# Sixteen of 22 gate/up pairs of a SwiGLU layer computed with Strassen's seven block products

## The chip, the cores and the metric

One NeuronCore of a Trainium2 chip. The metric is the device time of one execution in microseconds; three runs of the kernel before took 2012.99, 2013.51 and 2014.62 us, median 2013.51. All arithmetic is fp32. A product of two fp32 matrices is made on TensorE from three float32r matmuls: each operand is split into a high part and a rest, and high x high, high x rest and rest x high are summed.

## The reference, cut to what matters

Two layers of an encoder for 544 tokens (512 prompt frames and 32 sample frames) of width 1024. Each layer has a mixer (short convolution, latent attention, gated merge) and then the feed-forward part that the change touches:

```
x = x + rmsnorm(m, norm_attn_post)
gu = rmsnorm(x, norm_ffn_pre) @ w_gate_up            # (544 x 1024) @ (1024 x 5632)
f = (silu(gu[..., :2816]) * gu[..., 2816:]) @ w_down # (544 x 2816) @ (2816 x 1024)
x = x + rmsnorm(f, norm_ffn_post)
```

## The kernel before, in words

Activations lie transposed: features on the 128 partitions, tokens along the free axis, in two halves `hf` of 272 tokens (TH). 1024 features are 8 blocks of 128. A weight tile is 128 output features by 1024 inputs: 128 partitions x 1024 fp32, 512 KB. SyncE (SP) loads it into a `raw` buffer (two of them, in turn, L132), ScalarE (ACT) casts it to its high part (L129) and VectorE (DVE) subtracts to get the rest (L130); both parts are one `w` tile (L135, a ring of three, or one of the 17 big buffers of the tag "b", L78, of up to 8704 bytes per partition each).

One *unit* is one output block of 128 features for one half: `dense` (L188) issues 8 blocks x 3 matmuls = 24 matmuls of 128x128 by 128x272 (`mm3`, L183) into one PSUM bank. In this part of the kernel `psd` (L102) goes through seven banks in turn.

The order in the code: `tail(..., "mg", ...)` (L1039) makes 16 units of the merge product, eight for each half. When a half is complete, its chain `post_chain` (L317) starts: the norm over the merge product, the residual (`xb`), the unnormalised operand pair gh/gl (L341, L347), and at the end the second norm factor, which goes into `r2` (L367 to L370; then `hf` is in `ready`). The chain's steps are taken inside the following units (`step`, twice per unit of 24 matmuls), so its VectorE work stands between theirs and its few small matmuls (L237, L256) stand in TensorE's queue between units.

The gate/up part (L1066 to L1094) runs 22 pairs i, a pair being a gate tile and an up tile, each for both halves: 88 units. The first GR = 4 pairs run for half 0 and then for half 1; from there on each pair runs for both. TensorE uses the unnormalised operand; the factor r2 is multiplied in when PSUM is read: `gate` (L1046: multiply by r2, Silu), `up` (L1052: multiply by r2, multiply by the up product, cast to the high part), `low` (L1060: the rest). Units that end before their half's factor is ready are held in PSUM (`held`). `tick` (L169) after every unit splits a weight tile that has landed and has SP load the next one from the list `feed`. The results `ff` are the split operands of the down product, in groups of 8, 8 and 6 blocks.

Then `tail(..., "dn", DW, ...)` (L1102) makes 16 units of the down product, each of 22 blocks x 3 = 66 matmuls, in the order (0,0), (0,1), (1,0), ... of (m, half), reads each bank with two ScalarE instructions (square for the norm, L215, and multiply by the gain, L992), and starts the same kind of chain.

SP, GpSimd (POOL) and TensorE run in the order of the code; so do ScalarE and VectorE from L1028 on (`manual_schedule`). POOL has no work in the gate/up part beside four DMAs that store the residual (L336).

Of the kernel before, what the change touches and what calls it, by code (L numbers as in the profile page):

```python
# [33 lines left out]
def kernel(  # L34
# [67 lines left out]
    def psd(n=512):  # L102
        tag = "d"
        if wide[0]:
            tag = "dstdstd"[turn[0] % 7]
            turn[0] += 1
        return bank(tag)[:, :n]

    def f32(ap):
        return ap.bitcast(F32)  # L110
# [203 lines left out]
        stages(NW, scale, low)  # L314
        return hi, lo

    def post_chain(pre_l, pre_key, m, acc, xb, x_dst, gaps, hf, full=None, raw=None, scales=None):  # L317
        def pause(i):
            for _ in range(gaps[i]):
                yield  # L320

        yield from pause(0)
        d = rsqrt_cols([(acc, FS, EPS)])[0]
        yield from pause(1)
        r = bcast(d)
# [124 lines left out]
    for l in range(NL):  # L450
# [516 lines left out]
                dve.tensor_add(sg[hf], sg[hf], tg[hf][:, m, :])  # L967
                split(mxb[hf][0][:, m, :], mxb[hf][1][:, m, :], sg[hf])

        def tail(units, key, widths, rhs, l, post_key, pre_l, pre_key, x_src, x_dst, gaps, outs):  # L970
            mres = [blk([P, NC, TH], F32, "m") for _ in range(2)]
            accs = [Acc(), Acc()]
            ws = {}
            left = [NC, NC]
            for n, (m, hf) in enumerate(units):
                left[hf] -= 1
                ps = psd(TH)
                for pi, wdt in enumerate(widths):
# [24 lines left out]

        done = set()
        last = l == NL - 1
        GR = 4
        DW = (1024, 1024, 768)

        def after(*u):
            return lambda: u in done  # L1010

        def w_g(j, gate):
            return ("gu", j), w_gu[l, j], 1024, gate

# [5 lines left out]
        feed += [w_g(j, None) for j in range(2 * GR, 2 * FFC)]  # L1020
        for m in (0, 1, 2, 3, 4, 5, 6, 7, 5):
            feed += w_d(m, None if m != 6 else after("dn", 3, 0))
        if not last:
            feed += [(("in", l + 1, m), w_in[l + 1, m], 1024, after("dn", 7, 0) if m < 8 else None) for m in range(10)]
# [7 lines left out]
        for _ in range(3):  # L1032
# [2 lines left out]
        load_next()  # L1035
        now[0] += 1
        units = [(m, hf) for hf in range(2) for m in range(8)]
        h2, ready = {}, set()
        tail(units, "mg", (1024,), lambda hf, pi: mxb[hf], l, "attn_post", l, "ffn_pre",  # L1039
                  lambda hf: xs[hf], lambda hf: x_mid[l][hf], GM,  # L1040
                  [dict(raw=h2, scales=(r2, ready))] * 2)

        ff = [[(blk([P, n, TH], F32R, "fh"), blk([P, n, TH], F32R, "fl")) for n in (8, 8, 6)] for _ in range(2)]
        wg, held, sls, lows = {}, [], {}, []

        def gate(i, hf, ps):  # L1046
            sl = small([P, TH], s="sl")
# [4 lines left out]
        def up(i, hf, ps):  # L1052
            sl = sls[(i, hf)]
            dve.tensor_mul(sl, sl, r2[:, hf, :])
            dve.tensor_mul(sl, sl, ps)  # L1055
            fh, fl = ff[hf][i // 8]
            act.copy(fh[:, i % 8, :], sl)  # L1057
            lows.append((fl[:, i % 8, :], sl, fh[:, i % 8, :]))

        def low():  # L1060
            while lows:
                o, x, hi = lows.pop(0)
                dve.tensor_sub(o, x, f32(hi))

        runs = [(i, hf) for hf in range(2) for i in range(GR)] + [(i, hf) for i in range(GR, FFC) for hf in range(2)]
        for n, (i, hf) in enumerate(runs):  # L1066
            while hf not in h2:
                step()
            pss = []
            for u in range(2):  # L1070
                if (i, u) not in wg:
                    wg[(i, u)] = claim(("gu", 2 * i + u))
                ps = psd(TH)
                dense(ps, wg[(i, u)], h2[hf], NC)
                if hf == 1 and not 3 <= 2 * i + u < 2 * GR:
                    free[0] += 1
                low()
                pss.append(ps)
                if hf in ready:
                    while held:  # L1080
                        a = held.pop(0)
                        gate(a[0], a[1], a[2][0])
                        up(a[0], a[1], a[2][1])
                        low()
# [6 lines left out]
                tick()  # L1091
            if (i, hf) not in sls:
                held.append((i, hf, pss))
        low()  # L1094
# [7 lines left out]
        tail(units, "dn", DW, lambda hf, pi: ff[hf][pi], l, "ffn_post", l + 1, None if last else "attn_pre",  # L1102
             lambda hf: x_mid[l][hf], lambda hf: y_out[hf] if last else x_end[hf], GD, outs)
        if last:
            drain()
            vec.__exit__(None, None, None)
# [94 lines left out]
```

## Time and profile before

| | |
|---|---|
| median of the runs | 2013.51 us |
| profiled execution, its time | 2012.29 us |
| its span | 2010.4 us |
| TensorE busy | 1980.8 us, 15516 matmuls |
| VectorE, ScalarE, GpSimd busy | 1130.5, 826.1, 86.1 us |
| DMA | 190.89 MB, mean 95 GB/s |

Busy times are sums over the span; a matmul's record overlaps the next one's, so the pace of TensorE is read from the starts of matmuls and not from the durations (about 290 ns) of the records. A line number in a row can be a helper's: L129/L130 are all splits, L184 to L186 all matmul triples. A timeline row gives start, duration, engine, line and, in brackets, the idle time before it and what ended that.

### The profile page before, as it was taken

How to read it: one execution, taken by the hardware profiler on the slowest of the kernel's cores; microseconds unless marked ns; L12 is line 12 of the kernel's file. 1: busy time of each engine (PE TensorE's matmuls, PEld its weight loads, DVE VectorE, ACT ScalarE, POOL GpSimd, SP SyncE). 2: the span in 40 equal slices, each digit the busy share in tenths (PEclk: the TensorE clock that was granted, in tenths of full speed). 3: DMA queues.
4: the chain of work that ended last, by engine and by line, in shares of the span. 5: the costliest groups of instructions: out<-in, count | busy, mean ns of one | idle time of the engine just before them, and what ended most of it. 6: DMA issues, size and time to landing. Idle time of an engine off the chain costs nothing.

```text
span 2010.4 us, 37143 instructions
## 1 busy us (share of the span) xinstructions
PE 1980.8 (99%) x15516; PEld 1958.1 (97%) x15516; DVE 1130.5 (56%) x2318; ACT 826.1 (41%) x1676; POOL 86.1 (4%) x212
## 2 busy tenths in 40 slices
PE   8999999999999999999999999999999999999997
PEld 8999999999999999999999999999999999999997
DVE  7877776534457444432568777854344664444234
ACT  5455555612353222322445555555123533222231
POOL 0100000000000000000100100100000000000000
PEclk9999999999999999999999999999999999999999
DMA  5122222222342222223532222222223412222233
GB/s 194 63 77 68 69 82 69 92 98 85 112 154 87 79 91 85 85 88 88 193 106 78 75 69 72 81 91 79 85 94 119 158 55 93 87 94 83 79 107 135
DMA packets 58887, 190.89 MB, mean 95 GB/s; under 512 B 7968, under 2 KB 9664, under 8 KB 58592
## 3 DMA queue, kind: packets, MB, share of 16 engines
q1 hardware_dynamic: 49104, 163.58, 24.2%
q0 software_dynamic: 8320, 22.66, 3.5%
q8 instruction: 121, 1.98, 0.4%
q10 hardware_dynamic: 1296, 2.29, 0.3%
q14 instruction: 46, 0.38, 0.1%
HBM read 174.11 MB, written 10.20 MB: 92 GB/s over the span
## 4 chain that ended last, share of the span: by engine, by line
PE 92%; DVE 4%; DMA 1%; ACT 1%; issue 1%; DVEq 0%; SPq 0%; ACTq 0%
PE ps_d L184 16%; PE ps_d L186 16%; PE ps_d L185 16%; PE ps_s L184 7%; PE ps_s L186 7%; PE ps_s L185 7%; PE ps_t L184 6%; PE ps_t L186 6%; PE ps_t L185 6%; PE ps_t L755 2%; DMA raw<-in_w_in 1%; PE ps_v L770 1%; DVE w L130 1%; PE ps_v L771 1%; ACT w L129 1%
## 5 line engine op out<-in xcount | busy, mean ns | idle before, releaser
L130 DVE TENSOR_TENSOR w<-raw,w 128x1024 fp32r<-128x1024 f32 (+4 forms) x317 | 363.8, 1148 | 442.6 <-ACT w L129 441.2
L129 ACT CAST w<-raw 128x1024 fp32r<-128x1024 f32 (+4 forms) x317 | 312.1, 986 | 271.1 <-PE ps_d L186 98.6
L184 PE MATMUL ps_d<-hh,w 128*128 128x272 f32 x1096 | 320.0, 292 | 1.3 <-DVE v L130 1.3
L185 PE MATMUL ps_d<-hl,w 128*128 128x272 f32 x1096 | 317.0, 289 | 0.8 <-DVE hl L311 0.8
L186 PE MATMUL ps_d<-hh,w 128*128 128x272 f32 x1096 | 317.3, 290 | 0.0
L184 PE MATMUL ps_d<-gh,w 128*128 128x272 f32 x704 | 206.3, 293 | 6.1 <-DVE w L130 6.0
L184 PEld LDWEIGHTS ps_d<-hh,w 128*128 128x128 f32 x1096 | 206.9, 189 | 3.0 <-PE ps_d L186 1.7
L185 PEld LDWEIGHTS ps_d<-hl,w 128*128 128x128 f32 x1096 | 206.8, 189 | 2.0 <-DVE hl L311 1.3
L186 PEld LDWEIGHTS ps_d<-hh,w 128*128 128x128 f32 x1096 | 206.6, 189 | 0.0
L186 PE MATMUL ps_d<-gh,w 128*128 128x272 f32 x704 | 204.7, 291 | 0.0
L185 PE MATMUL ps_d<-gl,w 128*128 128x272 f32 x704 | 203.8, 289 | 0.0
L184 PEld LDWEIGHTS ps_d<-gh,w 128*128 128x128 f32 x704 | 133.5, 190 | 6.7 <-DVE w L130 6.5
L184 PE MATMUL ps_t<-gh,w 128*128 128x272 f32 x464 | 135.0, 291 | 0.0
L186 PE MATMUL ps_t<-gh,w 128*128 128x272 f32 x464 | 134.2, 289 | 0.0
L185 PEld LDWEIGHTS ps_d<-gl,w 128*128 128x128 f32 x704 | 133.8, 190 | 0.0
L185 PE MATMUL ps_t<-gl,w 128*128 128x272 f32 x464 | 133.6, 288 | 0.0
L186 PEld LDWEIGHTS ps_d<-gh,w 128*128 128x128 f32 x704 | 133.5, 190 | 0.0
L184 PE MATMUL ps_s<-gh,w 128*128 128x272 f32 x432 | 125.4, 290 | 0.1
L186 PE MATMUL ps_s<-gh,w 128*128 128x272 f32 x432 | 125.0, 289 | 0.0
L185 PE MATMUL ps_s<-gl,w 128*128 128x272 f32 x432 | 124.4, 288 | 0.0
L1049 ACT ACTIVATE sl<-sl 128x272 f32<-128x272 f32 x88 | 38.0, 432 | 182.1 <-DVE sl L1048 182.1
L1057 ACT CAST fh<-sl 128x272 fp32r<-128x272 f32 x88 | 36.9, 420 | 160.5 <-DVE sl L1055 160.5
(331 smaller groups left out, 5343.0 us busy)
## 6 DMA issues: line engine op xcount, KB each, us to landing
raw<-in_w_in SPq DMA_DIRECT2D x91, 512.0 KB, 3.3
raw<-in_w_gu SPq DMA_DIRECT2D x88, 512.0 KB, 3.2
raw<-in_w_mix SPq DMA_DIRECT2D x48, 512.0 KB, 3.2
raw<-in_w_dn SPq DMA_DIRECT2D x36, 512.0 KB, 3.6
raw<-in_w_dn SPq DMA_DIRECT2D x18, 384.0 KB, 3.0
raw<-in_w_b SPq DMA_DIRECT2D x16, 320.0 KB, 2.9
x_mid<-xb POOLq DMA_DIRECT2D x16, 272.0 KB, 2.3
xb<-x_mid POOLq DMA_DIRECT2D x16, 272.0 KB, 4.7
```

What stands on the lines that cost most here:

```text
L129: act.copy(hi, src)
L130: dve.tensor_sub(lo, src, f32(hi))
L184: pe.matmul(ps, lhsT=wlo, rhs=xhi, start=first, stop=False)
L185: pe.matmul(ps, lhsT=whi, rhs=xlo, start=False, stop=False)
L186: pe.matmul(ps, lhsT=whi, rhs=xhi, start=False, stop=last)
L755: pe.transpose(pt[:, o * P : o * P + P], probs[qt][:, kt * P : kt * P + P], ident)
L770: pe.matmul(out, lhsT=both, rhs=ptl[:, b, o : o + 256], start=kt == 0, stop=False)
L771: pe.matmul(out, lhsT=both, rhs=pth[:, b, o : o + 256], start=False, stop=kt == nkt - 1)
L1049: act.activation(sl, sl, AF.Silu)
L1057: act.copy(fh[:, i % 8, :], sl)
```

## The change

For 16 of the 22 pairs of each layer (i = 6 to 21; GN = 6), the four units of a pair (gate and up, two halves) are seen as one product of 2 x 2 blocks: outputs (gate, up) x (half 0, half 1), summed over two halves k0, k1 of the 1024 features. Eight block products of 4 blocks x 3 matmuls become seven, with sums of operand blocks made beforehand and sums of results made afterwards (the variant with shared sums).

- Operands x: `x_forms` makes the normalised operand in place in `xb` (kept by `keep`), from it four sums T1 to T4, and splits seven blocks of 128 x 4 x 272 (B11, B21, B22, T1 to T4) once per layer, in steps that are put behind the units of the first pairs from run n = 3 on, two steps per unit.
- Weights: `w_load(b)` has SP load six 256 KB blocks for a pair (four into a buffer `ra`, one into half a raw buffer, one into `u1`), and POOL add to three of them by accumulating DMAs; the third of these reads what the first has written. `produce` splits them to 3.5 `w` tiles of 1024 columns for the next pair; one more sum is made by VectorE. The load for a pair is issued two to three pairs ahead.
- Results: one copy, seven VectorE additions or subtractions of 272 columns from PSUM, one Silu and one multiplication of 544 columns per pair, in place of gate/up/low. Results are kept unsplit in `fx` and split later: four splits of 544 columns in the last pair, the other seven of half 0 ahead of the first down unit, all eleven of half 1 ahead of the second (`f_splits`, called by `tail` through `before`).
- The loads of the down weights are issued in the last two pairs; before, `tick` issued them.
- The first six pairs run as before, without `low` and with their product written to `fx`.

```diff
-        GR = 4
+        GR, GN = 4, 6
+        fx = [blk([P, 4, 2, TH], F32, "fx") for _ in range((FFC + 3) // 4)]
         def up(i, hf, ps):
             sl = sls[(i, hf)]
             dve.tensor_mul(sl, sl, r2[:, hf, :])
-            dve.tensor_mul(sl, sl, ps)
-            fh, fl = ff[hf][i // 8]
-            act.copy(fh[:, i % 8, :], sl)
-            lows.append((fl[:, i % 8, :], sl, fh[:, i % 8, :]))
+            dve.tensor_mul(fx[i // 4][:, i % 4, hf, :], sl, ps)
+        def form(name, k, src):
+            if name not in xf:
+                xf[name] = blk([P, 2, 4, TH], F32R, "xf")
+            hi, lo = xf[name][:, 0, k : k + 2, :], xf[name][:, 1, k : k + 2, :]
+            act.copy(hi, src)
+            while later:
+                later.pop(0)()
+            later.append(lambda: dve.tensor_sub(lo, src, f32(hi)))
+        def w_load(b):
+            def src(u, half):
+                return w_gu[l, 2 * (GN + b) + u, :, 512 * half : 512 * half + 512]
+            ra = blk([P, 2048], F32, "ra")
+            g0, s3, s2, s1 = [ra[:, o : o + 512] for o in range(0, 2048, 512)]
+            nc.sync.dma_start(s1, src(1, 0))
+            nc.sync.dma_start(s3, src(1, 0))
+            nc.sync.dma_start(s2, src(0, 0))
+            nc.sync.dma_start(g0, src(0, 0))
+            nc.gpsimd.dma_start(s1, src(1, 1), accum_op=ALU.add)
+            nc.gpsimd.dma_start(s3, src(0, 0), accum_op=ALU.add)
+            nc.gpsimd.dma_start(s2, s1, accum_op=ALU.add)
+            rb = rawp.tile([P, 1024], F32, tag=ring("raw", 2), name=nm("raw"))
+            nc.sync.dma_start(rb[:, 0:512], src(0, 1))
+            u1 = tmp([P, 512], s="u1")
+            nc.sync.dma_start(u1, src(1, 1))
+        def produce(n):
+            b, j = n // 4, n % 4
...
+            if j == 2:
+                dve.tensor_add(rb[:, 512:1024], ra[:, 1024:1536], rb[:, 0:512])
+            src = (ra[:, 0:1024], ra[:, 1024:2048], rb, u1)[j]
+            wd = 512 if j == 3 else 1024
+            w = wt[n] = w_tile(n % 5 < 2 or b == NB - 1)
+            act.copy(w[:, 0, :wd], src)
+            while wlater:
+                wlater.pop(0)()
+            wlater.append(lambda: dve.tensor_sub(w[:, 1, :wd], src, f32(w[:, 0, :wd])))
...
+            if j == 2 and b + 2 < NB:
+                w_load(b + 2)
+        order = ("B11", "T3", "T2", "T1", "B21", "B22", "T4")
+        for b in range(NB):
+            i = GN + b
+            sl, up2 = tmp([P, 2, TH], s="slp"), tmp([P, 2, TH], s="upp")
+            for f in range(7):
+                n = 4 * b + f // 2
+                ps = banks[f] = psd(TH)
+                w, o = wt[n], 512 * (f % 2)
+                x = xf[order[f]]
+                for k in range(4):
+                    s = slice(o + k * P, o + k * P + P)
+                    mm3(ps, w[:, 0, s], w[:, 1, s], x[:, 0, k, :], x[:, 1, k, :], k == 0, k == 3)
+                if f == 0:
+                    act.copy(sl[:, 0, :], ps)
+                elif f == 2:
+                    dve.tensor_sub(sl[:, 1, :], sl[:, 0, :], ps)
+                    dve.tensor_add(up2[:, 0, :], sl[:, 1, :], banks[1])
...
+                elif f == 5:
+                    dve.tensor_add(sl[:, 1, :], sl[:, 1, :], ps)
+                    act.activation(sl, sl, AF.Silu)
+                elif f == 6:
+                    dve.tensor_add(up2[:, 0, :], up2[:, 0, :], ps)
+                    dve.scalar_tensor_tensor(fx[i // 4][:, i % 4, :, :], up2, -1.0, sl, op0=ALU.mult, op1=ALU.mult)
+                if f in (1, 3, 5, 6):
+                    produce(n + 4)
...
+        def f_splits(m, hf):
+            while todo and todo[0][0] == hf:
+                f_split(*todo.pop(0))
```

## Rows read from the trace of the kernel before

**Rows 1.** The page: span, then busy time, share and instructions of each engine.
```profile
span 2010.4 us, 37143 instructions
PE 1980.8 (99%) x15516; PEld 1958.1 (97%) x15516; DVE 1130.5 (56%) x2318; ACT 826.1 (41%) x1676; POOL 86.1 (4%) x212
```
**Rows 2.** Waits of TensorE: who, for whom, us in total, times, longest.
```profile
PE ps_d L184 <- DVE w L130: 6.0, 1, 6.0
...
PE ps_v L256 <- DVE y L250: 2.5, 2, 1.9
```
**Rows 3.** Windows: gate/up part of layer 0 (busy us of each engine, PEclk, DMA share, GB/s).
```profile
597.00:870.00 273.00, 273.00 (x2170) 273.00 (x2169) 139.98 (x270) 87.17 (x151) 2.17 (x4) 1.00 0.25 87
```
**Rows 4.** Timeline of TensorE: two units' first matmuls, a chain's transposes, the down part's start.
```profile
601.96 0.29 PE L184 MATMUL ps_d<-gh,w 128*128 128x272 f32 x1
...
604.99 0.29 PE L184 MATMUL ps_s<-gh,w 128*128 128x272 f32 x1
...
640.26 0.49 PE L256 MATMUL ps_v<-ident,y 128*128 128x128 f32 x3
...
867.58 0.29 PE L184 MATMUL ps_s<-fh,w 128*128 128x272 f32 x1
```
**Rows 5.** Groups by line and form on VectorE: count, busy us, mean ns, idle before.
```profile
L130 DVE TENSOR_TENSOR w<-raw,w 128x1024 fp32r<-128x1024 f32 x263 | 322.0, 1225 | 418.9 <-ACT w L129 417.5
...
L347 DVE SCALAR_TENSOR_TENSOR gl<-xb,gn,gh 128x272 fp32r<-128x272 f32 x40 | 18.2, 495 | 0.0
...
L1055 DVE TENSOR_TENSOR sl<-sl,ps_d 128x272 f32<-128x272 f32 x39 | 17.1, 438 | 14.7 <-PE ps_d L186 12.4
...
L130 DVE TENSOR_TENSOR xl<-at,xh 128x544 fp32r<-128x544 f32 x16 | 10.7, 714 | 12.4 <-ACT xh L129 12.4
...
L130 DVE TENSOR_TENSOR w<-raw,w 128x512 fp32r<-128x512 f32 x8 | 5.5, 688 | 0.0
```
**Rows 6.** The same on ScalarE.
```profile
L129 ACT CAST w<-raw 128x1024 fp32r<-128x1024 f32 x263 | 274.9, 1046 | 247.4 <-PE ps_d L186 78.8 <-PE ps_t L186 45.7 <-PE ps_s L186 40.9
L1049 ACT ACTIVATE sl<-sl 128x272 f32<-128x272 f32 x88 | 38.0, 432 | 182.1 <-DVE sl L1048 182.1
...
L129 ACT CAST xh<-z 128x544 fp32r<-128x544 f32 x16 | 9.2, 642 | 0.0
...
L129 ACT CAST w<-raw 128x512 fp32r<-128x512 f32 x8 | 5.0, 621 | 3.7 <-PE ps_d L186 3.7
```
**Rows 7.** Timeline of VectorE after the second half's chain, layer 0.
```profile
626.53 0.43 DVE L1063 TENSOR_TENSOR fl<-sl,fh 128x272 fp32r<-128x272 f32 x1
...
634.20 0.15 DVE L239 TENSOR_SCALAR v<-ps_d 128x3 f32<-128x3 f32 x1
```
**Rows 8.** DMA queues in 681:850 (169 us): packets, MB, share of 16 engines.
```profile
q1 hardware_dynamic: 4011, 14.64, 25.0%
```
**Rows 9.** DMA queues in 584:609 (25 us), where POOL's DMAs run too.
```profile
q1 hardware_dynamic: 797, 2.94, 33.3%
q0 software_dynamic: 640, 2.23, 24.1%
```
**Rows 10.** DMA issues over the span: queue, count, KB each, median us to landing.
```profile
raw<-in_w_gu SPq DMA_DIRECT2D x88, 512.0 KB, 3.2
...
xb<-x_mid POOLq DMA_DIRECT2D x16, 272.0 KB, 4.7
...
xb<-in_x POOLq DMA_DIRECT2D x8, 272.0 KB, 3.8
...
raw<-in_w_a SPq DMA_DIRECT2D x8, 256.0 KB, 2.8
```
**Rows 11.** Timeline of POOL: the issue of a DMA.
```profile
619.13 0.55 POOL L336 DMA_DIRECT2D x_mid<-xb  x1 [0.72 <-DVE xb L335]
```
**Rows 12.** Timeline of ScalarE at the end of the first down unit.
```profile
876.11 0.40 ACT L215 ACTIVATE sq<-ps_s 128x272 f32<-128x272 f32 x1 [6.16 <-PE ps_s L186]
876.40 0.48 ACT L992 ACTIVATE m<-ps_s,gn 128x272 f32<-128x272 f32 x1
```
**Rows 13.** Windows: near the span's end, TensorE with a gap (columns as in rows 3).
```profile
1995.00:2000.00 5.00, 3.64 (x29) 3.34 (x27) 0.77 (x3) 0.78 (x2) 0.00 (x0) 1.00 0.00 0
```

More of the change, by code (lines that the diff above doesn't have):

```diff
@@ L315, in norm_split, with post_chain @@
         return hi, lo
-    def post_chain(pre_l, pre_key, m, acc, xb, x_dst, gaps, hf, full=None, raw=None, scales=None):
+    def post_chain(pre_l, pre_key, m, acc, xb, x_dst, gaps, hf, full=None, raw=None, scales=None, keep=None):
         def pause(i):
@@ L367, in post_chain @@
         if raw is not None:
+            if keep is not None:
+                keep[hf] = xb
             t, r = r, scales[0][:, hf, :]
@@ L968, with tail @@
                 split(mxb[hf][0][:, m, :], mxb[hf][1][:, m, :], sg[hf])
-        def tail(units, key, widths, rhs, l, post_key, pre_l, pre_key, x_src, x_dst, gaps, outs):
+        def tail(units, key, widths, rhs, l, post_key, pre_l, pre_key, x_src, x_dst, gaps, outs, before=None):
             mres = [blk([P, NC, TH], F32, "m") for _ in range(2)]
@@ L977, in tail @@
                 ps = psd(TH)
+                if before is not None:
+                    before(m, hf)
                 for pi, wdt in enumerate(widths):
@@ L1019 @@
         feed += [w_g(j, None) for j in range(3)] + [w_g(j, after("mg", j, 1)) for j in range(3, 2 * GR)]
[L1020 to L1024, printed above, removed]
+        feed += [w_g(j, None) for j in range(2 * GR, 2 * GN)]
         xs = x0 if l == 0 else x_end
@@ L1037 @@
         units = [(m, hf) for hf in range(2) for m in range(8)]
-        h2, ready = {}, set()
+        h2, ready, keep = {}, set(), {}
         tail(units, "mg", (1024,), lambda hf, pi: mxb[hf], l, "attn_post", l, "ffn_pre",
                   lambda hf: xs[hf], lambda hf: x_mid[l][hf], GM,
-                  [dict(raw=h2, scales=(r2, ready))] * 2)
-        ff = [[(blk([P, n, TH], F32R, "fh"), blk([P, n, TH], F32R, "fl")) for n in (8, 8, 6)] for _ in range(2)]
-        wg, held, sls, lows = {}, [], {}, []
+                  [dict(raw=h2, scales=(r2, ready), keep=keep)] * 2)
+        fx = [blk([P, 4, 2, TH], F32, "fx") for _ in range((FFC + 3) // 4)]
+        wg, held, sls = {}, [], {}
         def gate(i, hf, ps):
@@ L1054, in up @@
             dve.tensor_mul(sl, sl, r2[:, hf, :])
-            dve.tensor_mul(sl, sl, ps)
-            fh, fl = ff[hf][i // 8]
-            act.copy(fh[:, i % 8, :], sl)
-            lows.append((fl[:, i % 8, :], sl, fh[:, i % 8, :]))
[L1060 to L1065, printed above, removed]
+            dve.tensor_mul(fx[i // 4][:, i % 4, hf, :], sl, ps)
@@ new lines, with x_forms, quarter @@
+        xf = {}
+        later = []
+        def form(name, k, src):
[6 more added lines that the diff above has]
+            later.append(lambda: dve.tensor_sub(lo, src, f32(hi)))
+        def x_forms():
+            def quarter(hf, half, k):
+                return keep[hf][:, 4 * half + k : 4 * half + k + 2, :]
+            for hf in range(2):
+                while hf not in ready:
+                    yield False
+                for half in range(2):
+                    for k in (0, 2):
+                        q = quarter(hf, half, k)
+                        for e in range(2):
+                            c = 4 * half + k + e
+                            dve.scalar_tensor_tensor(q[:, e, :], q[:, e, :], g(l, "ffn_pre", c), r2[:, hf, :],
+                                                     op0=ALU.mult, op1=ALU.mult)
+                        if hf == 0 or half == 1:
+                            form(("B11", "B21", "", "B22")[2 * hf + half], k, q)
+                        yield True
+            b11, b21, b12, b22 = [lambda k, hf=hf, half=half: quarter(hf, half, k) for hf in range(2) for half in range(2)]
+            for name, o, x, y, op in (("T1", b11, b11, b12, ALU.subtract), ("T3", b12, b22, b12, ALU.subtract),
+                                      ("T2", b22, b22, b11, ALU.add), ("T4", b21, b22, b21, ALU.subtract)):
+                for k in (0, 2):
+                    dve.tensor_tensor(o(k), x(k), y(k), op=op)
+                    form(name, k, o(k))
+                    yield True
+            while later:
+                later.pop(0)()
@@ new lines @@
+        NB = FFC - GN
+        wt, rws = {}, {}
+        wlater = []
+        def w_load(b):
[14 more added lines that the diff above has]
+            nc.sync.dma_start(u1, src(1, 1))
+            rws[b] = ra, rb, u1
@@ new lines, in produce @@
+        def produce(n):
+            b, j = n // 4, n % 4
+            if b >= NB:
+                return
+            ra, rb, u1 = rws[b]
+            if j == 2:
[7 more added lines that the diff above has]
+            wlater.append(lambda: dve.tensor_sub(w[:, 1, :wd], src, f32(w[:, 0, :wd])))
+            if n == 4 * NB - 1:
+                wlater.pop(0)()
+            if j == 2 and b + 2 < NB:
+                w_load(b + 2)
@@ L1066 @@
+        runs = [(i, hf) for hf in range(2) for i in range(GR)] + [(i, hf) for i in range(GR, GN) for hf in range(2)]
+        xg = x_forms()
+        xdone, xq = [False], [0]
         for n, (i, hf) in enumerate(runs):
@@ L1076 @@
                     free[0] += 1
-                low()
                 pss.append(ps)
@@ L1083 @@
                         up(a[0], a[1], a[2][1])
-                        low()
                     if u == 0:
@@ L1091 @@
                 tick()
+                d = 2 * n + u - 4 * GR
+                if n >= GR - 1:
+                    for _ in range(2):
+                        if next(xg, None) is None:
+                            break
+                if d == 1:
+                    w_load(0)
+                if d == 5:
+                    w_load(1)
+                if d in (3, 5, 6, 7):
+                    produce(xq[0])
+                    xq[0] += 1
             if (i, hf) not in sls:
                 held.append((i, hf, pss))
-        low()
+        for _ in xg:
+            pass
@@ new lines, with f_split @@
+        while chains:
+            step()
+        for m in (0, 1, 2, 3, 4, 5, 6, 7, 5):
+            feed += w_d(m, None if m != 6 else after("dn", 3, 0))
+        if not last:
+            feed += [(("in", l + 1, m), w_in[l + 1, m], 1024, after("dn", 7, 0) if m < 8 else None) for m in range(10)]
+        ff = [[(blk([P, n, TH], F32R, "fh"), blk([P, n, TH], F32R, "fl")) for n in (8, 8, 6)] for _ in range(2)]
+        def f_split(hf, gi, k):
+            s = slice(k, k + 2)
+            split(ff[hf][gi][0][:, s, :], ff[hf][gi][1][:, s, :], fx[2 * gi + k // 4][:, k % 4 : k % 4 + 2, hf, :])
@@ new lines @@
+        todo = [(hf, gi, k) for hf in range(2) for gi, n in enumerate((8, 8, 6)) for k in range(0, n, 2)]
+        order = ("B11", "T3", "T2", "T1", "B21", "B22", "T4")
+        for b in range(NB):
+            i = GN + b
+            sl, up2 = tmp([P, 2, TH], s="slp"), tmp([P, 2, TH], s="upp")
+            banks = {}
+            for f in range(7):
[11 more added lines that the diff above has]
+                    dve.tensor_add(up2[:, 0, :], sl[:, 1, :], banks[1])
+                elif f == 3:
+                    dve.tensor_add(up2[:, 1, :], up2[:, 0, :], ps)
+                    dve.tensor_add(sl[:, 1, :], sl[:, 1, :], ps)
+                elif f == 4:
+                    dve.tensor_add(sl[:, 0, :], sl[:, 0, :], ps)
+                elif f == 5:
+                    dve.tensor_add(sl[:, 1, :], sl[:, 1, :], ps)
+                    act.activation(sl, sl, AF.Silu)
[4 more added lines that the diff above has]
+                    produce(n + 4)
+                e = f if b == NB - 1 else -1
+                if b == NB - 2 and f in (4, 6) or e in (1, 4, 6):
+                    load_next()
+                if e in (0, 3, 5):
+                    split_next()
+                if e in (1, 2, 4, 5):
+                    f_split(*todo.pop(0))
@@ L1096 @@
+        free[0] = 0
+        def f_splits(m, hf):
+            while todo and todo[0][0] == hf:
+                f_split(*todo.pop(0))
         units = [(m, hf) for m in range(5) for hf in range(2)] + [(5, 0), (6, 0), (7, 0), (7, 1), (6, 1), (5, 1)]
@@ L1102 @@
         tail(units, "dn", DW, lambda hf, pi: ff[hf][pi], l, "ffn_post", l + 1, None if last else "attn_pre",
-             lambda hf: x_mid[l][hf], lambda hf: y_out[hf] if last else x_end[hf], GD, outs)
+             lambda hf: x_mid[l][hf], lambda hf: y_out[hf] if last else x_end[hf], GD, outs, f_splits)
         if last:
```

## The prediction, as it was put on record before the result

> **What bounds the kernel now.** I read the page's engine shares first: TensorE is busy 1980.8 of 2010.4 us, VectorE 56%, ScalarE 41% [rows 1]. Busy time alone doesn't say that TensorE sets the time, so the second view is TensorE's waits. The longest single wait is 6.0 us, at the start; after that none is over 1.9 us [rows 2]. Third, the stage that the change touches: in the gate/up part of layer 0 TensorE never pauses in 273 us, at a granted clock of 1.00 (2.4 GHz), with VectorE at 140.0 us (51%) and the DMA engines at a share of 0.25 [rows 3]; layer 1's window is the same within 1 us. So here a matmul removed is time removed, as long as nobody else becomes late. The price of a matmul comes from starts, not from the overlapping records: two units of 24 matmuls begin at 601.96 and 604.99, 3.03 us a unit, 0.126 us a matmul [rows 4].
>
> **The change part by part.**
>
> *Matmuls.* A pair is 4 units, 4 x 3.03 = 12.12 us. Afterwards it is seven products of 12 matmuls, each half a unit: 7 x 1.515 = 10.6 us. Saved: 1.515 us x 16 pairs x 2 layers = 48.5 us. Shape, operand kinds and bank rotation stay, so I take the same price per matmul. That is all the change can give.
>
> *VectorE and ScalarE in the pair loop.* Per pair VectorE has three rests of 1024 columns (3 x 1.225), a rest and a sum of 512 (2 x 0.688), seven 272-column operations on PSUM (7 x 0.438) and one of 544 columns (0.714): 8.8 us of 10.6 [rows 5]. Before it was 2 x 1.225 + 8 x 0.438 = 6.0 of 12.1. ScalarE has 3 x 1.046 + 0.621 + a copy (0.43) + a Silu of 544 columns (0.64) = 4.8 us [rows 6]. Neither is over, so the question is order. A `w` tile's rest is issued four to five products (6.1 us or more) before TensorE wants it. Walking one pair with these durations, TensorE at 1.515 us a product: the second tile's rest stands behind the additions of product 5 and ends 11.5 us after the pair's start, wanted at 13.6; the third ends at 13.8, wanted at 16.7; the first ends at 8.4, wanted at 10.6. So about 2 us to spare, a PSUM bank is read long before its turn comes again seven products later, and the cost is 0. If that cover went, TensorE would run at VectorE's pace (rival 2).
>
> *Operand forms.* Per layer, on VectorE 16 x 0.495 + 8 x 0.714 + 14 x 0.714 = 23.6 us [rows 5], on ScalarE 14 x 0.642 = 9.0 us [rows 6], put between the evictions of units 6 to 18 of the 24 that remain ahead of the pair loop (counted from 0), where TensorE has work of its own. The tight place is half 0's four steps behind units 6 and 7 (n = 3). They stand in VectorE's queue ahead of the small chain that half 1's second norm needs, which starts at 634.20 [rows 7] and takes 1.7 us; TensorE wants its result for the transposes at 640.26 [rows 4], and these can't be passed. The steps are 8 x 0.495 + 4 x 0.714 = 6.8 us; three `low` of 0.44 (one at 626.53 [rows 7]) and the two waits of half a microsecond before them go. End of the chain: 634.2 + 1.7 + 6.8 - 2.3 = 640.4 by mean durations, some 2 us sooner if back-to-back instructions overlap. Cost 0 to 1.6 us per layer; I take 0, because instructions that stand side by side on one engine do overlap in the trace, by 0.11 us in the one pair shown [rows 12]. From unit 12 on VectorE gets 2.2 to 4.9 us per 3.03 us unit and falls behind by at most 4 us; seven banks give it 18.
>
> *Weights.* SP moves 6 x 262 KB = 1.57 MB per pair instead of 1.05. At 14.64 MB in 25.0% of 169 us = 346 GB/s [rows 8] that is 4.5 us of all 16 DMA engines. The trace has no accumulating DMA. Lower end: the price of POOL's plain DMAs, 2.23 MB in 24.1% of 25 us = 370 GB/s [rows 9]: 0.79 MB in 2.1 us, together 6.6 of 10.6 us. Upper end: each has all engines for its whole time to landing, 4.7 us in the worst plain row [rows 10]: 14.1 us, together 18.6. I take twice the plain price, 4.2 us, since such a transfer has to read two operands where a plain one reads one and the row of POOL's plain DMAs is the nearest [rows 9]: 8.7 us per pair, 82% of the DMA engines, cost 0. Latency: load, first accumulation, accumulation on that one, 2.8 + 3.8 + 3.8 = 10.4 us by [rows 10], 14 if each is slowed to 4.7. The load is issued behind product 5 of one pair and wanted behind product 1 or 3 of the pair after next, 15 to 18 us later. POOL's issue is 3 x 0.55 us per pair [rows 11] on an idle engine. The waits that POOL gets hold up only its own next accumulation.
>
> The Trainium skill (DMA: Bandwidth & Descriptors, section Rules for kernel authors) says that an accumulating DMA reads its destination and writes it later, which is what the doubled price stands for; no run here shows it yet. The same page (section Anatomy of one DMA) gives each DMA a fixed 2.0 us beside its bytes. If the fixed part occupied the engines, nine DMAs of 262 KB would be an estimated 9 x 2.6 = 23 us a pair. The trace disagrees as far as plain loads go: a 512 KB load lands in 3.2 us, yet costs the engines 1.5 us by the rate above [rows 8].
>
> *Start of the down part.* Before, its operands were split long ahead. Now half 1's eleven splits stand behind the first down unit's two reads on ScalarE. That unit ends 8.31 us after its start, at 875.89 (867.58 plus 66 x 0.126), and ScalarE's reads of it end at 876.88 [rows 4, 12], 1.0 us later; then a cast (0.64) and a rest (0.71) must end before the second matmul of unit (0,1): 2.4 us of idle TensorE. From there a split covers 6 matmuls (0.76 us) and takes 0.64 to 0.71, so it keeps ahead. The next weight tile's split stands behind all eleven: 1.0 + 11 x 0.64 + 1.05 + 1.23 = 10.3 us after unit (0,0)'s end, unit (1,0) starts 2.4 + 8.3 = 10.7 after it: just in time. Half 0's seven splits run at 0.7 us each against 0.76 and start with 3 us of lead: 0. So 2.4 us x 2 layers = 4.8 us lost; ends 0 and 4 us per layer. The clock: the row nearest to such a gap has TensorE idle for 1.4 us and still at 1.00 [rows 13].
>
> *Sum*, against the profiled execution's 2012.29 us: -48.5 + 4.8 = -43.7, 1968.6 us. The median of the runs stands 1.2 us above that execution: **1970 us**.
>
> **Rivals.**
>
> 1 (slower). *Accumulating DMAs are several times dearer than plain ones and the DMA engines become the bound.* Place: the pair loop from the third pair on, when the lead of two pairs is used up: 14 pairs x 2 layers. At four times the plain price: 4.5 + 8.5 = 13.0 us per pair, 2.4 over 10.6, 67 us in all: 2037 us. It decides from 12.2 us per pair (43.7 / 28 over 10.6), an accumulation of 2.5 us, 3.6 times plain. For it: the operation is new here, and per-pair DMA time at least rises from 3.0 to 6.6 us. Against: plain DMAs leave the engines three quarters idle [rows 3].
>
> 2. *VectorE's order, not its sum, sets the pair's pace.* A 2 us margin is small when an instruction reads PSUM right behind TensorE. If a pair takes VectorE 11.3 us (8.8 of work, and 2.5 of waits that it can't fill, for the bank, for Silu and for the cast), 0.7 x 32 = 22 us are lost: 1992 us. For it: in the gate/up part VectorE's busy groups show waits of 0.3 us and more per instruction for ScalarE and TensorE [rows 5]. Against: in my walk it idles only once per pair, about 1 us.
>
> 3. *Fixed costs per DMA occupy the engines.* Worked from rows as a mechanism here: each 262 KB load taking its 2.8 us to landing in turn [rows 10] would give 6 x 2.8 = 16.8 us a pair before any accumulation, 6.2 over, 174 us lost: 2144 us. The page's fixed 2.0 us (above) is this case. The rate of 346 GB/s speaks against it [rows 8].
>
> **How the numbers follow.** My forecast has 0.67, its own range 1963 to 1978 (nothing lost at the down part, or 4 us per layer and 1.6 per layer in the forms). Rival 2, or a milder DMA bound that leaves a gain, 0.12: 1980 to 2006. Rival 1: 0.16, rival 3: 0.02; the rest, 0.03, lies near no change. Range 1962 to 2006, which leaves out about 0.2, nearly all of it above. A measurement of this kernel tells a difference from about 0.2%, 4 us. Faster 0.79, same 0.03, slower 0.18.
>
> **What will show it.** 384 matmuls fewer in each engine row and 0.126 us still between starts; TensorE's waits by name: `w` from VectorE or a DMA on `ra` in the pair loop (rivals 1 to 3), VectorE on `fl` at the second down unit, 2 to 3 us, twice. DMA share in the pair loop near 0.8; at 0.95 or more rival 1 has come true. VectorE near 85% there; above 95% it is rival 2. The prediction is wrong if the pair takes more than 10.8 us.

## The result, and the profile after

The changed kernel takes 1985.3 us (median of 4 runs, 1983.2 to 1990.3) against 2013.3 us before on the same chip (2012.8 to 2014.6): a ratio of 0.9864, 95% interval 0.9844 to 0.9883. It is faster, by 28 us. The forecast was 1970 us with a loss of 4.8 us against a gain of 48.5: the time lies in the range of 1962 to 2006, outside of the forecast's own 1963 to 1978. So 16 us of the forecast gain are to be found, or 20.5 us of the full 48.5. The profiled execution below is the slowest of the four, 1990.3 us with a span of 1988.5, so it shows some 5 us more of loss than the median.

The page of the changed kernel, span and engines (answers to [rows 1]):

```profile
span 1988.5 us, 37200 instructions
...
PE 1944.8 (98%) x15132; PEld 1919.9 (97%) x15132; DVE 1264.9 (64%) x2510; ACT 889.3 (45%) x1724; POOL 171.1 (9%) x308
```

The 384 matmuls are gone, yet TensorE's busy time fell by only 36.0 us and the span by 21.9. Busy time that doesn't fall with the count is matmuls that became longer, so the clock is to be looked at too. The same window as in [rows 3], and within it the pair loop alone, which runs from 679.86 to 849.35 (busy us of each engine, granted clock, DMA share, GB/s):

```profile
597.00:870.00 273.00, 267.19 (x2080) 266.10 (x2079) 210.00 (x369) 121.04 (x179) 44.47 (x52) 0.98 0.67 167
680.00:849.00 169.00, 169.00 (x1343) 169.00 (x1342) 130.28 (x209) 72.55 (x96) 36.10 (x41) 1.00 0.83 200
```

In the pair loop TensorE never pauses. The losses lie in front of it and behind it. TensorE's waits inside the window 597:870 (answers to [rows 2]):

```profile
PE ps_s L184 <- DVE w L130: 2.8, 1, 2.8
PE ps_s L184 <- ACT fh L129: 1.4, 1, 1.4
PE ps_d L185 <- DVE fl L130: 1.2, 2, 0.7
PE ps_s L185 <- DVE fl L130: 0.4, 1, 0.4
```

Layer 1 has the same four groups (2.9, 1.4, 1.1 and 0.4 us). Where the span's time went is read from the first matmul on each kind of operand: `gh` opens the gate/up part, `fh` the down part. In the timeline of TensorE, before:

```profile
598.94 0.29 PE L184 MATMUL ps_t<-gh,w 128*128 128x272 f32 x1
...
1594.90 0.29 PE L184 MATMUL ps_d<-gh,w 128*128 128x272 f32 x1
...
1863.53 0.29 PE L184 MATMUL ps_d<-fh,w 128*128 128x272 f32 x1
```

and after:

```profile
599.16 0.29 PE L184 MATMUL ps_t<-gh,w 128*128 128x272 f32 x1
...
849.35 0.29 PE L184 MATMUL ps_d<-fh,w 128*128 128x272 f32 x1
...
1585.68 0.29 PE L184 MATMUL ps_d<-gh,w 128*128 128x272 f32 x1
...
1835.86 0.29 PE L184 MATMUL ps_s<-fh,w 128*128 128x272 f32 x1
```

The differences of these starts (with 867.58 of [rows 4], and those of the experiments read in the same way) split each span into five stretches:

| us | to first gh | gate/up 0 | down 0 to gate/up 1 | gate/up 1 | down 1 to the end | span |
|---|---|---|---|---|---|---|
| before | 598.9 | 268.6 | 727.3 | 268.6 | 146.9 | 2010.4 |
| after | 599.2 | 250.2 | 736.3 | 250.2 | 152.6 | 1988.5 |
| e1_pace | 599.0 | 246.1 | 731.6 | 246.2 | 152.7 | 1975.5 |
| e2_early | 598.8 | 249.0 | 729.6 | 249.2 | 148.9 | 1975.5 |
| e3_both | 599.1 | 246.1 | 728.9 | 245.9 | 148.9 | 1968.9 |
| e4_fill | 600.1 | 247.7 | 731.4 | 247.7 | 151.1 | 1978.0 |
| e5_noacc | 598.3 | 249.1 | 734.7 | 248.8 | 151.1 | 1982.0 |

Each gate/up part should have become shorter by 16 x 1.515 = 24.2 us and became 18.4 shorter: 5.8 us lost per layer. The down parts grew by 9.0 and 5.8 us where 2.4 was forecast. The row of e5_noacc, an experiment below with the same order of work, is a second look at the changed kernel: that execution took 1983.8 us, near the median, and lost 4.7 and 4.4 us in the gate/up parts and 7.4 and 4.2 behind them.

**The place in the gate/up part.** The one wait on `w` from L130 is that of unit 21, the up tile of pair 5, the last but two of the ordinary units. ScalarE, VectorE and TensorE there (timelines; the bracket is the idle time before and its releaser):

```profile
665.32 0.43 ACT L1049 ACTIVATE sl<-sl 128x272 f32<-128x272 f32 x1 [0.34 <-DVE sl L1048]
665.66 1.03 ACT L129 CAST w<-raw 128x1024 fp32r<-128x1024 f32 x1
```
```profile
664.22 0.72 DVE L1067 TENSOR_TENSOR xf<-xb,xf 128x544 fp32r<-128x544 f32 x1
664.86 0.43 DVE L1048 TENSOR_TENSOR sl<-ps_s,r 128x272 f32<-128x272 f32 x1
666.72 1.23 DVE L130 TENSOR_TENSOR w<-raw,w 128x1024 fp32r<-128x1024 f32 x1 [1.43 <-ACT w L129]
```
```profile
658.96 0.29 PE L184 MATMUL ps_t<-gh,w 128*128 128x272 f32 x1
...
668.00 0.60 PE L184 MATMUL ps_s<-gh,w 128*128 128x272 f32 x1 [2.83 <-DVE w L130]
...
673.61 0.43 PE L184 MATMUL ps_t<-gh,w 128*128 128x272 f32 x1
```

Read from the bottom: unit 18 ends where the next one starts, at 658.96, but VectorE comes to read it only at 664.86, 5.9 us later, because the steps that make the operand forms (L1067 and the lines before it) stand ahead. ScalarE's Silu (L1049) waits for that, and in ScalarE's queue the cast of unit 21's weight tile stands behind the Silu. Then VectorE's rest of the tile must follow: TensorE waits 2.83 us. With ScalarE's cast, VectorE's rest and the two gate operations (1.03 + 1.23 + 0.43 + 0.43 = 3.1 us) the tile would have been ready at 665.17, where the unit before it ended, if VectorE had been 3.1 us late and not 5.9: the difference is the wait.

The wait isn't all. The 24 matmuls behind it last from 668.00 to 673.61, 5.6 us for 3.03. The windows there:

```profile
666.00:668.00 2.00, 0.00 (x0) 0.00 (x1) 1.28 (x2) 1.63 (x2) 0.21 (x1) 0.80 0.91 288
668.00:670.00 2.00, 2.00 (x9) 2.00 (x10) 1.72 (x4) 0.14 (x1) 1.55 (x2) 0.50 0.81 230
670.00:674.00 4.00, 4.00 (x19) 4.00 (x19) 0.60 (x2) 1.23 (x2) 0.00 (x0) 0.50 0.80 162
674.00:676.00 2.00, 2.00 (x18) 2.00 (x17) 1.42 (x2) 0.00 (x0) 0.12 (x1) 0.99 0.92 215
```

The granted clock falls to 0.50, the lower of TensorE's two levels (1.2 GHz), after TensorE had stood still, and returns at 674. That is 2.6 us more; 2.8 + 2.6 = 5.4 of the 5.8 lost in this execution.

**The place at the start of the down part.** TensorE's matmuls that waited, and ScalarE's queue that answers to [rows 12]:

```profile
852.40 0.39 PE L185 MATMUL ps_d<-fl,w 128*128 128x272 f32 x1 [0.49 <-DVE fl L130]
...
854.14 0.39 PE L185 MATMUL ps_d<-fl,w 128*128 128x272 f32 x1 [0.73 <-DVE fl L130]
...
860.97 0.39 PE L184 MATMUL ps_s<-fh,w 128*128 128x272 f32 x1 [1.40 <-ACT fh L129]
861.73 0.58 PE L185 MATMUL ps_s<-fl,w 128*128 128x272 f32 x1 [0.37 <-DVE fl L130]
```
```profile
859.60 0.40 ACT L215 ACTIVATE sq<-ps_d 128x272 f32<-128x272 f32 x1 [4.51 <-PE ps_d L186]
859.90 0.48 ACT L996 ACTIVATE m<-ps_d,gn 128x272 f32<-128x272 f32 x1
860.27 6.11 ACT L129 CAST fh<-fx 128x544 fp32r<-128x544 f32 x11
```

By the starts of the matmuls around them the two `fl` waits on half 0's splits cost 1.5 us and the pair at 861 costs 2.2 us. The latter is the forecast step, mechanism and size (2.4). The former was costed at nothing. After it, too, the clock is at half for a while:

```profile
862.00:864.00 2.00, 2.00 (x10) 2.00 (x10) 2.00 (x4) 2.00 (x5) 0.00 (x0) 0.50 0.00 0
864.00:866.00 2.00, 2.00 (x14) 2.00 (x13) 2.00 (x4) 2.00 (x5) 0.00 (x0) 0.70 0.04 8
```

From 861.73 to 865.24 stand 15 intervals that would take 1.9 us and took 3.5: 1.6 us. Together 5.3 us per layer.

**A third place.** What is left of layer 0's 9.0 us lies around the start of layer 1, where nothing was changed. From the third unit of the down part to the first `gh` of layer 1 it is 710.7 us before, 714.1 after and 714.0 in e5_noacc: 3.3 to 3.5 us lost in both. TensorE waits there once for 3.7 us on `y` (L256), where it waited 0.6 before, and the clock is at half twice (0.57 on average over 981:985 and over 1008:1012) where it was once before. In e1_pace to e4_fill the same stretch takes 710.6 to 711.2 us, although none of them edits it, in e6_moreacc and e7_more 712.1 and 712.5. Why it depends on the order of work ahead of it was not followed.

**DMA.** The queues in 700:820, where every pair loads for a later one (packets, MB, share of 16 engines; answers to [rows 8, 9]):

```profile
q1 hardware_dynamic: 9910, 18.04, 47.4%
q0 software_dynamic: 4803, 8.73, 44.6%
```

The accumulating queue moved 8.73 MB in 44.6% of 120 us, 163 GB/s, 2.27 times as dear as the plain 370 of [rows 9]; SP's loads ran at 317 GB/s for 346. The share is 0.92 in this stretch, and still TensorE has no wait in the pair loop, on a transfer or on a weight tile.

### The profile page after: what moved, and what is told of

Read it like the earlier page. It is cut to its first block, busy times and chain, and to the rows that moved or that the text cites. A ratio compares the mean times of both kernels' runs of the same rounds, so it can differ in the third digit from the quotient of the medians.

```text
span 1988.5 us, 37200 instructions
## 1 busy us (share of the span) xinstructions
PE 1944.8 (98%) x15132; PEld 1919.9 (97%) x15132; DVE 1264.9 (64%) x2510; ACT 889.3 (45%) x1724; POOL 171.1 (9%) x308
## 4 chain that ended last, share of the span: by engine, by line
PE 84%; DVE 10%; DMA 2%; ACT 2%; issue 2%; SPq 0%; DVEq 0%; ACTq 0%
PE ps_d L184 15%; PE ps_d L185 15%; PE ps_d L186 15%; PE ps_s L184 6%; PE ps_s L185 6%; PE ps_s L186 6%; PE ps_t L184 5%; PE ps_t L186 5%; PE ps_t L185 5%; PE ps_t L757 2%; DVE w L130 2%; DMA raw<-in_w_in 2%; ACT w L129 1%; PE ps_v L772 1%; PE ps_v L773 1%
## 5 line engine op out<-in xcount | busy, mean ns | idle before, releaser
L130 DVE TENSOR_TENSOR w<-raw,w 128x1024 fp32r<-128x1024 f32 (+5 forms) x253 | 285.4, 1129 | 328.1 <-ACT w L129 326.8
L129 ACT CAST w<-raw 128x1024 fp32r<-128x1024 f32 (+5 forms) x253 | 245.4, 971 | 269.8 <-PE ps_d L186 103.1
L184 PE MATMUL ps_d<-xf,w 128*128 128x272 f32 x384 | 111.3, 290 | 0.0
L186 PE MATMUL ps_d<-xf,w 128*128 128x272 f32 x384 | 111.1, 289 | 0.0
L185 PE MATMUL ps_d<-xf,w 128*128 128x272 f32 x384 | 110.6, 288 | 0.0
L744 ACT ACTIVATE pr<-ps_s,y 128x128 f32<-128x128 f32 (+3 forms) x128 | 67.6, 528 | 69.3 <-DVE y L741 67.4
L185 PE MATMUL ps_d<-fl,w 128*128 128x272 f32 x308 | 88.9, 289 | 1.2 <-DVE fl L130 1.2
L184 PE MATMUL ps_d<-fh,w 128*128 128x272 f32 x308 | 89.6, 291 | 0.0
L186 PE MATMUL ps_d<-fh,w 128*128 128x272 f32 x308 | 89.1, 289 | 0.0
L184 PE MATMUL ps_d<-gh,w 128*128 128x272 f32 x248 | 73.8, 298 | 6.2 <-DVE w L130 6.2
L1132 DVE TENSOR_TENSOR w<-ra,w 128x1024 fp32r<-128x1024 f32 x64 | 78.0, 1219 | 0.0
L184 PE MATMUL ps_s<-xf,w 128*128 128x272 f32 x256 | 74.2, 290 | 0.0
L184 PE MATMUL ps_t<-xf,w 128*128 128x272 f32 x256 | 74.2, 290 | 0.0
L186 PE MATMUL ps_s<-xf,w 128*128 128x272 f32 x256 | 74.1, 289 | 0.0
L186 PE MATMUL ps_t<-xf,w 128*128 128x272 f32 x256 | 74.1, 289 | 0.0
```

The costliest lines, as they stand in the source:

```text
L129: act.copy(hi, src)
L130: dve.tensor_sub(lo, src, f32(hi))
L184: pe.matmul(ps, lhsT=wlo, rhs=xhi, start=first, stop=False)
L185: pe.matmul(ps, lhsT=whi, rhs=xlo, start=False, stop=False)
L186: pe.matmul(ps, lhsT=whi, rhs=xhi, start=False, stop=last)
L744: act.activation(pr[:, :nk], ps[:, :nk], AF.Exp, bias=mx, accum_out=sm)
```

## The experiments

My theory after this reading: two queue positions cost two waits per layer, each followed by half clock, and the DMAs cost nothing. The main rival: the accumulating DMAs, with which the engines are at 0.92, delay something that the waits don't show. The experiments ran on two chips on which the kernel before took 2014.2 to 2014.4 us, 1 us more than above, and four runs of one kernel spread over 2 to 7 us, so the differences of medians below are good to some 3 us.

**e1_pace: the forms later.** Two form steps per unit from the time on that their inputs are there become a written-out map by unit.

```
+PACE = {6: 2, 7: 2, 12: 2, 13: 2, 14: 2, 15: 2, 16: 1, 18: 2, 19: 1, 20: 1}
-if n >= GR - 1:
-    for _ in range(2):
-        if next(xg, None) is None:
-            break
+for _ in range(PACE.get(2 * n + u, 0)):
+    next(xg, None)
```

> Theory A: the gain is lost at two places per layer, each a wait of TensorE and then a stretch at half clock. Place 1 is the up tile of pair 5, whose split stands behind operand forms in VectorE's queue: 2.8 us of wait and 24 matmuls at 0.227 us for 0.126, 2.4 us more. Here the forms leave room (one step behind unit 16, none behind 17, the rest behind 18 to 20), so the wait goes: about 2 x 5.2 = 10 us less than the changed kernel, 1975 us, with place 2 unchanged. Rival B: TensorE only meets here what the pair loop's DMAs and VectorE would make it wait for anyway; the first pairs' weights then come late, since xb's buffer comes free some 5 us later, and the time stays within 3 us of the changed kernel.

1977.4 us (1976.1 to 1980.4), ratio to before 0.9819 [0.9804, 0.9833]: 7.8 us off the changed kernel's median, nearer to theory A than to B. TensorE's waits in 597:870, the window at unit 21, and ScalarE ahead of the new wait:

```profile
PE ps_t L184 <- DVE w L1132: 1.4, 1, 1.4
PE ps_s L184 <- ACT fh L129: 1.4, 1, 1.4
```
```profile
668.00:672.00 4.00, 4.00 (x34) 4.00 (x33) 3.52 (x7) 2.87 (x4) 0.55 (x1) 1.00 0.61 176
```
```profile
686.79 1.05 ACT L1129 CAST w<-ra 128x1024 fp32r<-128x1024 f32 x1 [3.82 <-DMA ra<-ra]
```

The wait of unit 21 and its half clock are gone; each gate/up part is 4.0 us shorter than in the changed kernel's profile, and 2.6 to 3.0 shorter than in e5_noacc's. The other part of the 7.8 us lies at the third place, which this edit doesn't touch. A smaller wait takes the old one's place: L1132 is the rest of a pair's weight tile, here of pair 1. Its loads are issued at 667.94, 6.0 us ahead of the pair loop, where the changed kernel issues them 15.5 us ahead (664.38), and by the trace's releaser its cast waits for the landing of the third accumulating DMA (`ra<-ra`). So with the forms later, TensorE does wait behind a pair's DMAs, 1.4 us a layer.

**e2_early: half 1's splits ahead of the first down unit.**

```
-if e in (1, 2, 4, 5):
+if e in (1, 2, 3, 4):
     f_split(*todo.pop(0))
 ...
-while todo and todo[0][0] == hf:
+while todo:
     f_split(*todo.pop(0))
```

> Theory A: place 2 is the start of the down part: 3.0 us of waits for fl and fh and a stretch at half clock after them, about 2 us. Here all splits stand ahead of the first down unit's eviction on ScalarE, and the four of the last pair one product earlier: 2 x 4 to 5 us less, 1975 to 1977 us, with place 1 unchanged. Rival B: the splits are bound by VectorE's total work there, so the wait moves to the next weight tile: under 3 us less.

1978.5 us (1975.7 to 1980.3), ratio 0.9822 [0.9806, 0.9839]: 6.7 us off, for the 8 to 10 of theory A. The `fh` wait and the clock's fall behind it are gone, one `fl` wait of 1.5 us stays, where there had been two of 1.2 together (597:870):

```profile
PE ps_s L184 <- DVE w L130: 2.9, 1, 2.9
PE ps_d L185 <- DVE fl L130: 1.5, 1, 1.5
```

**e3_both: both edits.**

> Both edits. Theory A: the effects add, since the places lie 170 us apart: 1985 - 10 - 9 = 1966 us, near 2012 - 48.5 + 1.2 = 1965, the full price of 384 matmuls. Rival B: under 6 us less than the changed kernel.

1972.0 us (1969.7 to 1974.8), ratio 0.979 [0.9776, 0.9805]: 13.3 us off, nearly the sum of the two (14.5), though not the 1966 that I expected. What remains in 597:870 is

```profile
PE ps_d L185 <- DVE fl L130: 1.4, 1, 1.4
PE ps_t L184 <- DVE w L1132: 1.4, 1, 1.4
```

so the two edits bring back 13 of the 20.5 us that were missing from the full 48.5 (4.8 of the 20.5 had been forecast as lost), and each leaves a smaller wait behind. The third place's share is in the gains of both single edits, so that it counts twice in the 14.5. What this version still lacks, by its row in the table, is 1.7 and 1.5 us in the gate/up parts and 1.6 and 2.0 behind them. It is faster than both kernels.

**e4_fill: unused matmuls in the gaps.** The changed kernel with its waits left in, and TensorE kept at work in front of them.

```
+if (n, u) == (10, 1):
+    for q in range(22): pe.matmul(px, ...)     # result unused
 ...
+if (m, hf) == (0, 1):
+    for q in range(11): pe.matmul(px, ...)     # result unused
```

> The changed kernel with matmuls that no result uses, put where TensorE waits: 22 (2.8 us) ahead of the second unit on the up tile of pair 5's predecessor place, that is ahead of unit 21, and 11 (1.4 us) ahead of the down unit (0,1). If the half clock comes from TensorE standing idle, the waits are filled, the clock stays at 2.4 GHz and 2.4 us at place 1 and up to 2 us at place 2 come back per layer: 6 to 9 us less than the changed kernel, 1977 to 1979 us. If the clock falls for another reason, the fillers give nothing or cost up to 4.2 us per layer: 1985 to 1993 us.

1978.7 us (1977.5 to 1979.9), ratio 0.9823 [0.9808, 0.9837]: 6.6 us faster with 66 matmuls more. The filled gap in TensorE's timeline, and a window in the place where the changed kernel was at 0.50:

```profile
665.97 2.93 PE L1152 MATMUL ps_v<-gh,w 128*128 128x272 f32 x22
669.10 0.39 PE L184 MATMUL ps_s<-gh,w 128*128 128x272 f32 x1 [0.20 <-DVE w L130]
```
```profile
668.00:672.00 4.00, 3.80 (x31) 3.58 (x30) 3.26 (x6) 1.77 (x3) 1.73 (x2) 1.00 0.82 208
```

Unit 21 comes no sooner relative to its weights; only the clock stays at 2.4 GHz. So at this place it is TensorE's standing still that brings the half clock about. The 6.6 us are not all from the two places: in the table e4_fill has 2.5 us less than the changed kernel in each gate/up part, but of its 4.9 us less behind the first one 3.4 lie at the third place. That the gain is the clock's, wherever it fell, the mean granted clocks of all runs bear out: 0.990, 0.993, 0.994 and 0.995 in the changed kernel's four, 0.996 to 0.997 in e4_fill's. The difference of the means, 0.0035 of 1985 us, makes an estimated 7 us.

**e5_noacc: the accumulation's price.** `accum_op=ALU.add` is struck from the three DMAs.

> The three accumulating DMAs of each pair become plain ones of the same sizes on the same queue; the sums of weights that they made are left out, so the output is another one. My theory (their 2.26-fold price lies beside TensorE work, and no wait of the pair loop is on a transfer): the GpSimd queue's share of the DMA engines in the pair loop falls from 42 to about 20%, the total from 84 to about 65%, TensorE stays without a wait in the loop, and the time stays within 4 us of the changed kernel's 1985. Rival (the accumulating DMAs cost part of the missing 16 us, by their load on the DMA engines or by GpSimd's longer issues): 1970 to 1978 us.

1985.4 us (1983.6 to 1987.9), ratio 0.986 [0.9844, 0.9877]: the changed kernel's time to within 1 us. The same stretch as above, 700:820:

```profile
q1 hardware_dynamic: 9504, 17.31, 43.7%
q0 software_dynamic: 2815, 9.24, 21.8%
```

The queue's price halves (9.24 MB in 26.2 us, 353 GB/s), the total falls from 0.92 to 0.66, and the time stays: as the changed kernel orders its work, the accumulating DMAs cost nothing that the runs can tell. The rival falls.

**e6_moreacc: two more accumulating DMAs per pair.**

```
+nc.gpsimd.dma_start(g0, src(1, 1), accum_op=ALU.add)
+nc.gpsimd.dma_start(s3, src(1, 1), accum_op=ALU.add)
```

> Two more accumulating DMAs of 256 KB per pair (five for three); the output is another one. They add 2 x 1.6 us of all 16 DMA engines to a pair, from 0.84 x 10.6 = 8.9 to 12.1 us, more than the 10.6 us that a pair's matmuls last. If the price by throughput (164 GB/s, worked out from the queue's share) is right, the weights of the later pairs come late: TensorE waits on the weight splits by name in the pair loop, about 1.5 us a pair, 14 pairs a layer less what the lead of two pairs hides (some 8 us): 10 to 15 us a layer, 2005 to 2016 us. Rival (the share shown for accumulating packets is largely waiting for the memory, and engines have room for other packets beside them): within 5 us of 1985.

1993.9 us (1991.5 to 1995.9), ratio 0.9898 [0.9884, 0.9913]: 8.6 us slower than the changed kernel, below the 20 to 31 of the one theory and above the 5 of the other. 700:820 as a window, and the new wait of layer 0's pair loop:

```profile
700.00:820.00 120.00, 118.75 (x938) 118.08 (x937) 89.30 (x145) 50.22 (x67) 47.73 (x54) 1.00 1.07 260
```
```profile
PE ps_d L184 <- DVE w L1134: 1.1, 1, 1.1
```

The engines are full (the share counts overlapping packets, so it can pass 1) and now TensorE does wait on a pair's weights (L1134 is the line of L1132 here), 1.1 us in layer 0 and 2.3 in layer 1. The full engines moved 260 GB/s; a pair of 11 x 262 KB = 2.88 MB then needs 11.1 us, 0.5 over the pair's 10.6, not the 1.5 that adding the queues' prices gave. Over 14 pairs that is 7 us a layer, most of it hidden by the lead of two pairs. The gate/up parts are 2.0 and 3.1 us longer than the changed kernel's (252.2 and 253.3 us), 5 of the 8.6 us; the rest was not assigned. The two more DMAs also lengthen the chain that a pair's weights wait for, and the run doesn't tell that from full engines. So a bound by the DMAs, as in rival 1, was not far away with three accumulations: by the share, 8% of the engines.

**e7_more: two more splits of half 0 in the last pair but one,** on top of e3_both.

```
-if e in (1, 2, 3, 4):
+if e in (1, 2, 3, 4) or b == NB - 2 and f in (1, 3):
     f_split(*todo.pop(0))
```

> As the version with both edits (forms paced by the map, splits ahead of the first unit of the down part), and two more of half 0's splits in the last pair but one. VectorE's run of splits at the start of the down part (11.5 us for 18) is two splits of 0.7 us shorter. My theory: the one wait on fl that is left there (1.4 us a layer) goes or falls under 0.3 us, 2 x 1.4 us in all: 1969 us against 1972. Rival (the two splits only push back the down part's first weight split, or the pair's own VectorE work): 1971 to 1974, and a wait on w by name at the first units of the down part.

1972.4 us (1971.5 to 1973.9), ratio 0.9792 [0.9776, 0.9808], no gain over e3_both. The wait on `fl` fell from 1.4 only to 1.0 us per layer, so I was wrong that VectorE's run of splits alone makes it; the 0.4 us are below what the runs tell apart. The rival's second half is what the trace shows: VectorE's last addition ahead of the last pair's Silu (L1219) starts 0.07 us behind the down part's first matmul in e3_both (845.23 and 845.16) and 1.20 behind it here (846.06 and 844.86), so the splits that follow come later too. The wait on `w` that the rival also named did not come.

## Why the prediction was right, and where it wasn't

- *Matmuls: right.* The count fell by 384 and the pair loop runs without a wait: 169.5 us for 16 pairs, 10.59 a pair for the 10.6 forecast and the 10.8 that would have refuted it.
- *VectorE in the pair loop, cost 0: right*, and rival 2 didn't come. VectorE is busy 77% there and not 85%: 130.3 / 169 x 10.6 = 8.2 us a pair for the 8.8 worked out from single durations, since instructions side by side overlap (664.22 and 664.86 above are 0.64 apart at a duration of 0.72).
- *Weights, cost 0: right.* The guess of twice the plain price was 2.27 times, 4.7 us a pair for 4.2, and the plain loads 5.0 for 4.5, over 700:820; 0.92 of the engines there, 0.83 over the whole loop, for the 0.82 forecast. e5_noacc shows no cost that the runs can tell, e6_moreacc how near the bound was. The rule of the Trainium skill (DMA: Bandwidth & Descriptors, section Rules for kernel authors) that an accumulating DMA reads its destination and writes it later agrees with the doubled price (163 GB/s with the accumulation, 353 without it in e5_noacc). Rival 3 is excluded: nine DMAs of 262 KB a pair fit into 10.6 us.
- *Operand forms, cost 0: the step that failed.* Half 0's steps cost nothing, as forecast (the transposes of [rows 4] begin at 640.47, no wait). But "falls behind by at most 4 us; seven banks give it 18" looked at the wrong cover. The lag was 5.9 us, and what it ran out of wasn't banks: a cast for TensorE's next weight tile stood in ScalarE's queue behind a Silu that waits for VectorE, which leaves 3.1 us. This cost 5.4 us per layer in the profiled execution and at most 4.4 to 4.7 in e5_noacc's, for 0 to 1.6 forecast; e1_pace removes it.
- *Start of the down part: mechanism right, size half.* Half 1's splits cost 2.2 us for the 2.4 forecast, and the next weight tile came in time. "Half 0's seven splits ... with 3 us of lead: 0" was wrong, 1.5 us: VectorE had a 768-column weight rest and the last pair's own two operations ahead of them, and that rest itself waited 1.45 us for a cast behind the last pair's Silu. e2_early removes the larger part.
- *The clock, priced at nothing: wrong.* The forecast read [rows 13] as a gap of 1.4 us at full clock. The row doesn't show that: its 1.4 us are a gap of 0.96 us and the first 0.4 of another, of 1.92, and the window ends before the clock falls. In the 2 us from 2002 on it is 0.53. The same trace had a plain case against it at the start of layer 1. TensorE's timeline at both places, and a window, all before:

```profile
1011.18 0.83 PE L237 MATMUL ps_d<-ones,acc 128*128 128x1 f32 x6 [1.53 <-DVE acc L224]
...
1998.78 0.83 PE L237 MATMUL ps_t<-ones,acc 128*128 128x1 f32 x6 [0.96 <-DVE acc L224]
2001.53 0.51 PE L256 MATMUL ps_v<-ident,y 128*128 128x128 f32 x3 [1.92 <-DVE y L250]
```
```profile
1012.00:1016.00 4.00, 4.00 (x22) 4.00 (x22) 1.53 (x2) 3.12 (x6) 0.00 (x0) 0.57 0.39 118
```

In the profiled execution the half clock made 4.2 of the 10.7 us per layer at the two places (2.6 and 1.6). Its mean granted clock, 0.990, is the lowest of the four, so the median lost less.

- *The start of layer 1, not in the forecast:* 3.3 to 3.5 us once, cause open.

In sum 48.5 - 2 x (5.4 + 5.3) = 27 us, less 3.5 at the start of layer 1: 23.6, and the profiled execution gained 22.0 (2012.29 to 1990.31). The median's 28 comes from executions that lost less to the clock. Of the 10.7 us per layer only 2.2 stood in the forecast. That the time lies in the stated range is luck: the part from 1980 to 2006 stood there for rival 2 and for a milder DMA bound, and neither came.

## What to carry to other kernels

When work is inserted on an engine that has time to spare, work out for each queue behind it which instruction feeds the bound engine next and how late that may be; spare buffers of one kind say nothing of the other kinds. Price a wait of the bound TensorE with the slower clock behind it, up to as much again in this kernel and in some executions nothing, and look at where a new stage starts and ends before its steady state. A resource at 0.92 can be free of cost: take its load away in an experiment before you blame it, and ask again when other waits are gone: in e1_pace the same DMAs ended a wait. A gap in a window of the profile can be several, and the clock can fall behind the window's end, so read the single gaps and what follows them.

## What the runs showed of the hardware that was not expected

After the wait of 2.8 us the clock was at 0.50 for some 6 us in both layers of the changed kernel; in e2_early and e5_noacc, with the same wait in layer 0, it was back earlier (0.64 and 0.65 on average over 668:672). After the 1.4 us wait at the down part it depended: in e1_pace the same waits (1.40 and 0.37 us) left layer 0 at full clock and layer 1 at half, as two windows show:

```profile
860.00:864.00 4.00, 4.00 (x34) 4.00 (x33) 4.00 (x7) 3.38 (x6) 0.00 (x0) 1.00 0.02 4
...
1836.00:1838.00 2.00, 2.00 (x11) 2.00 (x11) 2.00 (x4) 2.00 (x4) 0.00 (x0) 0.50 0.00 0
```

So a wait of this length has no fixed price. An accumulating DMA costs GpSimd more to issue, 876 to 1013 ns by line, than a plain one, 545 to 555 ns (547 and 548 for the same three without the accumulation in e5_noacc). One of the three groups by line and form on GpSimd, in the changed kernel:

```profile
L1111 POOL DMA_DIRECT2D ra<-in_w_gu x32 | 32.4, 1013 | 7.7 <-DMA ra<-in_w_gu 6.7 <-issue 0.8
```
